# Sixteen bytes: where the high and low weight buffers of a float32r kernel begin in SBUF

## The chip, the cores and the metric

The kernel runs on one core of a Trainium2 chip. The metric is the device time of one execution in microseconds; the time before is the median of three runs, and a separate profiled execution gives the trace that is read here.

## The reference

Two transformer-like networks run one after the other on 256 tokens of width 1,024. Nearly all of the arithmetic is in plain matrix products of activations with float32 weights that are read once:

```python
def swiglu(x, w_gate, w_up, w_down):
    return (jax.nn.silu(x @ w_gate) * (x @ w_up)) @ w_down

def first_block(x, ...):
    for l in range(DEPTH):
        h = rms_norm(x, ffn1_norm[l])
        x = x + 0.5 * swiglu(h, ffn1_w_gate[l], ffn1_w_up[l], ffn1_w_down[l])
        h = rms_norm(x, mix_norm[l])
        ... = jnp.split(h @ w_in[l], SPLIT_POINTS, axis=-1)
        ...
        x = x + merged @ w_out[l]
        h = rms_norm(x, ffn2_norm[l])
        x = x + 0.5 * swiglu(h, ffn2_w_gate[l], ffn2_w_up[l], ffn2_w_down[l])
    return x

def second_block(x, c, ctx, ...):
    for i in range(DEPTH):
        ...
        if i % 2 == 0:
            y_c, y_l = even_mixer(h_c, h_l, ev_w_in[j], ev_w_out[j], ...)
        else:
            y_c, y_l = retention_mixer(h_c, h_l, od_w_in[j], od_w_out[j], ...)
        x = x + g_a * y_l
        x = x + g_m * sq_relu_mlp(modulate(rms_norm_2(x, norm_mlp_g[i]), sh_m, sc_m), mlp_w1[i], mlp_w2[i])
        ...
    return rms_norm_2(x, final_g)
```

## The kernel before, in words

A float32 product is made of three products in the type float32r, which TensorE reads at one column a step: every float32 number is split into a high part (the number rounded to float32r) and a low part (what is left), and high times high, high times low and low times high are added up in PSUM.

Weights come in pieces of 512 KB. `wload` (line 238) takes a raw buffer `wraw` and two split buffers `whi` and `wlo` from `wtile` (line 225), loads the raw piece by DMA from the queue of SyncE (line 246), and splits it: ScalarE copies it to `whi` (line 251), VectorE subtracts and writes `wlo` (line 252; a few pieces go to GpSimd). Each of the three buffers holds 1,024 float32 numbers a partition, 4,096 bytes, as 2 rows of 512 columns or as 4 rows of 256. There are four raw buffers and three of each split kind in the pool `wp`; the feed-forward and mixer stages add some of their own (`more_weights`).

Two routines multiply. In `gemm` (line 264) the weights are the moving operand, which streams through the array, and 128 columns of the activations (`hA`, `hB`, `ahi`, `alo`, `yhi`, `ylo`) are the stationary operand, which is loaded first; its three products are lines 291, 292 and 293. In `gemm_t` (line 299) 128 columns of the weights are stationary and the activations move; its products are lines 333, 334 and 335. The retention mixer has three float32r products of its own without weights (lines 1484 to 1486).

Two small tiles, `gap0` (64 bytes, line 106) and `gap1` (224 bytes, line 110), are allocated between pools and never read. With them every float32r tile begins at a multiple of 256 bytes, and since a product takes its operands at whole rows of 2,048 or 1,024 bytes or at groups of 128 columns (512 bytes), both operands of all 9,816 float32r products in the program begin at a multiple of 256.

Products in full float32 are left over in the mixers: line 1289 multiplies tiles that begin 32 bytes behind a multiple of 256 (a tile of 32 bytes, `sink2`, stands ahead of them), and line 1465 tiles at a multiple of 256.

The first 16,384 bytes of every partition are kept by the program for DMAs that GpSimd issues (their scratch memory); the tiles follow behind them.

Of the kernel before, what the change touches and what calls it, by code (L numbers as in the profile page):

```python
# [11 lines left out]
F32 = mybir.dt.float32  # L12
F32R = mybir.dt.float32r
# [86 lines left out]
class Net:  # L100
# [125 lines left out]
    def wtile(self, name, shape):  # L226

        own = {"wraw": 4, "whi": 3, "wlo": 3}[name]
        more = self.more.get(name, 0)
        i = self.turn[name] = (self.turn.get(name, -1) + 1) % (own + more)  # L230
        pool, bufs = (self.wp, own) if i < own else (self.more_pool, more)
        return pool.tile(shape, F32 if name == "wraw" else F32R, name=name, bufs=bufs)

    def more_weights(self, pool=None, **k):
        self.more_pool, self.more, self.turn = pool, k, {}
# [1373 lines left out]


# [12 lines left out]
```

## Time and profile before

| | |
|---|---|
| runs | 2446.25, 2447.65 and 2445.13 us, median 2446.25 us |
| profiled execution | 2448.74 us, of which the span from the first to the last instruction is 2447.0 us |
| mean granted TensorE clock | 0.992 of full speed |
| TensorE matmul | busy 2379.9 us, 97% of the span, 11,941 records |
| VectorE, ScalarE, GpSimd | busy 63%, 45% and 6% |
| moved by DMA | 405.85 MB, 166 GB/s over the span |

An engine's busy time counts an instruction from its start to its end. Matmuls overlap, and a matmul record is longer than the time until the next one starts, so the rate of TensorE is read here from start to start (called the pitch), in the timeline, which lists instructions in order of time.

### The profile page before, as it was taken

The numbers are of one execution on the slowest core, as the hardware profiler recorded it, in microseconds if no ns is written. First come the engines' busy times: TensorE is split into PE (matmuls) and PEld (weight loads), VectorE is DVE, ScalarE is ACT, GpSimd is POOL, SyncE is SP. The second block draws the span as 40 slices with busy tenths as digits, with TensorE's granted clock in tenths as the row PEclk, the third lists the DMA queues.
The fourth block names the chain that finished last, engine by engine and source line by source line (L and its number), as shares of the span: only waits on it lengthen the run. The fifth ranks groups of instructions, "written<-read, shape, count | busy, mean of one in ns | idle before, by whom it ended". The sixth has DMA issues, their size and how long they took to land. (4 is left out here: it accounts for less than half of the span.)

```text
span 2447.0 us, 31298 instructions
## 1 busy us (share of the span) xinstructions
PE 2379.9 (97%) x11941; PEld 1924.1 (79%) x11941; DVE 1542.1 (63%) x2237; ACT 1107.5 (45%) x1715; POOL 145.1 (6%) x175
## 2 busy tenths in 40 slices
PE   9999999999999999999999999999999999999998
PEld 7887777778788867778887767788887888887996
DVE  5775677756767557685855765555534654565665
ACT  5444664544444456554543434331424433334543
POOL 2000100110000000000000001000001110110000
PEclk9999999999999999999999999999999999999999
DMA  8775536856777554586642122645432433344664
GB/s 273 249 254 183 165 121 196 265 168 211 241 215 225 174 164 140 163 277 186 218 146 90 53 86 69 193 167 170 141 99 86 140 103 104 112 129 138 198 182 137
DMA packets 212350, 405.85 MB, mean 166 GB/s; under 512 B 14830, under 2 KB 48365, under 8 KB 211688
## 3 DMA queue, kind: packets, MB, share of 16 engines
q1 hardware_dynamic: 207416, 391.77, 50.8%
q0 software_dynamic: 3776, 9.38, 1.2%
q10 hardware_dynamic: 1008, 2.70, 0.3%
q8 instruction: 94, 1.54, 0.3%
q14 instruction: 56, 0.46, 0.1%
HBM read 401.48 MB, written 4.67 MB: 166 GB/s over the span
## 5 line engine op out<-in xcount | busy, mean ns | idle before, releaser
L252 DVE TENSOR_TENSOR wlo<-wraw,whi 128x1024 fp32r<-128x1024 f32 (+1 forms) x617 | 750.8, 1221 | 588.1 <-ACT whi L251 585.9
L251 ACT CAST whi<-wraw 128x1024 fp32r<-128x1024 f32 (+1 forms) x622 | 649.1, 1046 | 952.5 <-PE acc L293 707.7
L291 PE MATMUL acc<-whi,hA 128*128 128x512 f32 (+1 forms) x1472 | 561.0, 381 | 1.8 <-ACT hA L378 0.8
L292 PE MATMUL acc<-wlo,hA 128*128 128x512 f32 (+1 forms) x1472 | 556.9, 378 | 0.3 <-DVE wlo L252 0.3
L293 PE MATMUL acc<-whi,hA 128*128 128x512 f32 (+2 forms) x1152 | 432.5, 375 | 1.4 <-DVE hA L379 1.4
L291 PEld LDWEIGHTS acc<-whi,hA 128*128 128x128 f32 x1472 | 278.1, 189 | 61.0 <-issue 8.6
L292 PEld LDWEIGHTS acc<-wlo,hA 128*128 128x128 f32 x1472 | 278.3, 189 | 49.1 <-DVE wlo L252 1.7
L291 PE MATMUL acc<-whi,ahi 128*128 128x512 f32 x736 | 288.5, 392 | 0.0
L293 PE MATMUL acc<-whi,alo 128*128 128x512 f32 x736 | 286.8, 390 | 0.0
L292 PE MATMUL acc<-wlo,ahi 128*128 128x512 f32 x736 | 286.7, 390 | 0.0
L333 PE MATMUL acc<-hA,whi 128*128 128x512 f32 (+1 forms) x752 | 259.5, 345 | 6.4 <-ACT rl L1385 3.4
L334 PE MATMUL acc<-hA,wlo 128*128 128x512 f32 (+1 forms) x752 | 259.2, 345 | 2.4 <-POOL wlo L252 2.4
L335 PE MATMUL acc<-hB,whi 128*128 128x512 f32 (+1 forms) x752 | 257.8, 344 | 0.0
L293 PEld LDWEIGHTS acc<-whi,hA 128*128 128x128 f32 x1152 | 218.0, 189 | 40.4 <-DVE hA L379 2.0
L333 PEld LDWEIGHTS acc<-hA,whi 128*128 128x128 f32 x752 | 144.8, 193 | 25.2 <-ACT rl L1385 3.8
L291 PEld LDWEIGHTS acc<-whi,ahi 128*128 128x128 f32 x736 | 138.2, 188 | 30.2 <-issue 2.3
L334 PEld LDWEIGHTS acc<-hA,wlo 128*128 128x128 f32 x752 | 145.1, 193 | 21.4 <-issue 3.4
L293 PEld LDWEIGHTS acc<-whi,alo 128*128 128x128 f32 x736 | 138.2, 188 | 29.3 <-issue 0.4
L292 PEld LDWEIGHTS acc<-wlo,ahi 128*128 128x128 f32 x736 | 138.2, 188 | 28.1 <-issue 0.2
L335 PEld LDWEIGHTS acc<-hB,whi 128*128 128x128 f32 x752 | 144.6, 193 | 17.2 <-issue 1.4
L999 DVE SCALAR_TENSOR_TENSOR hB<-hB,cT 128x1024 f32<-128x1024 f32 x112 | 141.0, 1279 | 22.1 <-DMA hB<-in_ada_w_dram 21.8
L293 PE MATMUL acc<-whi,hB 128*128 128x512 f32 (+1 forms) x320 | 121.5, 382 | 2.5 <-DVE hB L433 2.4
(422 smaller groups left out, 2544.2 us busy)
## 6 DMA issues: line engine op xcount, KB each, us to landing
wraw<-in_mlp_w_dram SPq DMA_DIRECT2D x128, 512.0 KB, 3.8
wraw<-in_ffn_w_gate_dram SPq DMA_DIRECT2D x88, 512.0 KB, 4.2
wraw<-in_ffn_w_up_dram SPq DMA_DIRECT2D x88, 512.0 KB, 4.6
wraw<-in_ffn_w_down_dram SPq DMA_DIRECT2D x88, 512.0 KB, 4.0
wraw<-in_w_in_dram SPq DMA_DIRECT2D x84, 512.0 KB, 3.7
hB<-in_ada_w_dram SPq DMA_DIRECT2D x64, 512.0 KB, 4.9
wraw<-in_od_w_in_dram SPq DMA_DIRECT2D x64, 512.0 KB, 3.7
xA<-in_ada_w_dram SPq DMA_DIRECT2D x32, 512.0 KB, 4.4
```

The lines of the kernel that those rows point to most:

```text
L251: nc.scalar.copy(hi[sl], raw[sl])
L252: (nc.gpsimd if e & 1 else nc.vector).tensor_sub(lo[sl], raw[sl], hi[sl].bitcast(F32))
L291: nc.tensor.matmul(o, h, wh, start=kt == first, stop=False)
L292: nc.tensor.matmul(o, h, wl, start=False, stop=False)
L293: nc.tensor.matmul(o, l, wh, start=False, stop=kt == end)
L333: nc.tensor.matmul(o, wh[:, cs], xh[:, kt, ts], start=st, stop=False, skip_group_check=skew_or_pair)
L334: nc.tensor.matmul(o, wl[:, cs], xh[:, kt, ts], start=False, stop=False, skip_group_check=skew_or_pair)
L335: nc.tensor.matmul(o, wh[:, cs], xl[:, kt, ts], start=False, stop=en, skip_group_check=skew_or_pair)
L999: nc.vector.scalar_tensor_tensor(acc[tok], raw, c, acc[tok], op0=ALU.mult, op1=ALU.add)
```

## The change

`wtile` no longer hands out a whole tile for `whi` and `wlo`. It allocates 1,088 float32 numbers a partition (4,352 bytes, 17 times 256), and gives the 1,024 that begin at the fifth: 16 bytes behind the tile's start. `wraw` and all activations stay as they were. Six split buffers stand in `wp`, and every further pair in a stage's pool, so the tiles behind them move by multiples of 256. The memory for this comes from the scratch for GpSimd's DMAs, which is halved to 8,192 bytes.

```diff
         pool, bufs = (self.wp, own) if i < own else (self.more_pool, more)
-        return pool.tile(shape, F32 if name == "wraw" else F32R, name=name, bufs=bufs)
+        if name == "wraw":
+            return pool.tile(shape, F32, name=name, bufs=bufs)
+
+        t = pool.tile([128, 1088], F32R, name=name, bufs=bufs)[:, 4:1028]
+        return t.rearrange("p (k n) -> p k n", k=shape[1])
...
-    nc = bacc.Bacc("TRN2", target_bir_lowering=False, num_devices=1)
+    nc = bacc.Bacc("TRN2", target_bir_lowering=False, num_devices=1, dynamic_dma_scratch_size=8192)
```

On every engine the same instructions stand in the same order as before, with the same shapes; addresses alone differ. Of the 9,816 float32r products, 7,392 (lines 291 to 293) now have the moving operand 16 bytes behind a multiple of 256 and the stationary one at a multiple, 2,256 (lines 333 to 335) have it the other way round, and 168 (lines 1484 to 1486) are as they were.

## Rows read from the trace of the kernel before

**Rows 1.** The page: busy time of the matmul engine, and the granted clock in 40 slices.
```profile
PE   9999999999999999999999999999999999999998
PEclk9999999999999999999999999999999999999999
```
**Rows 2.** Groups by line and shape, TensorE: busy us, mean ns of one, idle before.
```profile
L291 PE MATMUL acc<-whi,hA 128*128 128x512 f32 x1248 | 495.5, 397 | 1.7 <-ACT hA L378 0.8 <-ACT kv L1157 0.4 <-ACT whi L251 0.4
L291 PE MATMUL acc<-whi,ahi 128*128 128x512 f32 x736 | 288.5, 392 | 0.0
L291 PE MATMUL acc<-whi,yhi 128*128 128x512 f32 x256 | 101.4, 396 | 0.0
L333 PE MATMUL acc<-hA,whi 128*128 128x512 f32 x400 | 158.3, 396 | 3.4 <-ACT rl L1385 3.4
L333 PE MATMUL acc<-hA,whi 128*128 128x256 f32 x352 | 101.2, 288 | 3.0 <-ACT hA L432 3.0
L291 PE MATMUL acc<-whi,hA 128*128 128x256 f32 x192 | 55.7, 290 | 0.2
L291 PE MATMUL acc<-whi,hA 128*128 128x280 f32 x32 | 9.8, 305 | 0.0
```
**Rows 3.** Windows, line 291 alone: stretch, length, PE busy (count), PEld, PEclk, DMA, GB/s.
```profile
2304.00:2346.16 42.16, 24.12 (x62) 11.64 (x62) 1.00 0.63 195
```
**Rows 4.** Timeline of TensorE, 512 columns: start, length, line, operands; seven matmuls in turn.
```profile
152.97 0.39 PE L293 MATMUL acc<-whi,alo 128*128 128x512 f32 x1
...
154.33 0.39 PE L293 MATMUL acc<-whi,alo 128*128 128x512 f32 x1
```
**Rows 5.** Timeline of TensorE, 256 columns, weights stationary; seven matmuls in turn.
```profile
2349.86 0.28 PE L335 MATMUL acc<-hB,whi 128*128 128x256 f32 x1
...
2350.58 0.28 PE L335 MATMUL acc<-hB,whi 128*128 128x256 f32 x1
```
**Rows 6.** Timeline, full float32 of line 1289, and its durations by source line.
```profile
1431.55 2.74 PE L1289 MATMUL acc<-b,b 128*128 128x512 f32 x6
L1289 PE MATMUL acc<-b,b x32: 590/592/697, 1431.6 to 1455.8; 128*128 128x512 f32 x32
```
**Rows 7.** Timeline, 280 columns, first layer: six matmuls in turn.
```profile
284.38 0.30 PE L291 MATMUL acc<-whi,hA 128*128 128x280 f32 x1
...
285.05 0.30 PE L293 MATMUL acc<-whi,hA 128*128 128x280 f32 x1
```
**Rows 8.** Timeline, 280 columns, the same place of the second layer: seventeen in turn.
```profile
922.64 0.29 PE L292 MATMUL acc<-wlo,hA 128*128 128x280 f32 x1
...
924.69 0.29 PE L293 MATMUL acc<-whi,hA 128*128 128x280 f32 x1
```
**Rows 9.** Timeline, 512 columns behind other work of TensorE: eleven matmuls in turn.
```profile
230.81 0.40 PE L292 MATMUL acc<-wlo,hA 128*128 128x512 f32 x1
...
233.14 0.40 PE L293 MATMUL acc<-whi,hA 128*128 128x512 f32 x1
```
**Rows 10.** Who waited for whom: total us, times, longest us.
```profile
ACT whi L251 <- PE acc L293: 707.7, 375, 4.9
DVE wlo L252 <- ACT whi L251: 585.9, 378, 6.0
```
**Rows 11.** Groups by shape, ScalarE and VectorE, tiles at 256 and 32 bytes behind.
```profile
L479 ACT CAST ahi<-tp 128x512 fp32r<-128x512 f32 x40 | 23.5, 587 | 16.9 <-PE tp L477 15.8
L1235 ACT COPY b<-tp 128x512 f32<-128x512 f32 x16 | 9.4, 585 | 16.9 <-PE tp L1232 16.9
L1387 DVE TENSOR_TENSOR sq<-rl 128x512 f32<-128x512 f32 x48 | 32.9, 688 | 8.2 <-ACT rl L1385 7.6
L1266 DVE TENSOR_TENSOR b<-b,b 128x512 f32<-128x512 f32 x4 | 2.7, 683 | 0.0
```
**Rows 12.** The chain that ended last, by engine; GpSimd's largest DMA (KB, us to landing).
```profile
PE 39%; issue 4%; POOL 2%; DVE 2%; ACT 1%; DMA 1%; POOLq 0%; ACTq 0%; SPq 0%; DVEq 0%
bscratch<-bonce POOLq DMA_DIRECT2D x1, 2304.0 KB, 11.2
```

## The prediction

> **What bounds the kernel now.** I read the page first. TensorE is busy in every slice of the span and its clock is granted nearly throughout [rows 1]; it is the bound, and the other engines matter only where TensorE waits for them. The waits show the opposite: ScalarE's split of a weight piece waits 707.7 us for TensorE to give a buffer back, and VectorE waits for ScalarE [rows 10]. So the supply has slack, and what one multiplication takes is what the kernel takes.
>
> The groups by shape give the counts [rows 2]. With weights moving, line 291 has 1,248 + 736 + 256 = 2,240 products of 512 columns, 192 of 256 and 32 of 280; lines 292 and 293 have the same sums, which makes 6,720, 576 and 96, together 7,392. With weights stationary, line 333 has 400 of 512 and 352 of 256; with lines 334 and 335 it is 1,200 and 1,056, together 2,256. The change touches 7,392 + 2,256 = 9,648 products. Their busy times overlap, so the price of one is read from start to start. In one dense stretch line 291 stands 62 times in 42.16 us, 186 products with its two sisters: 226.7 ns each, at a granted clock of 1.00, which is 2.4 GHz [rows 3]. The timeline says the same, 1.36 us over 6 steps [rows 4]. For 256 columns it is 0.72 us over 6 steps, 120.0 ns [rows 5]. Together 7,920 × 0.2267 + 1,632 × 0.120 and the few of 280 are some 2,004 us of the 2,447 us span. **One nanosecond on each of 9,648 products is 9.65 us**; 0.2% of the time, about what a measurement of this kernel can tell from no change, is 4.9 us, half a nanosecond each.
>
> **What a product pays above its columns.** At 2.4 GHz 512 columns are 213.3 ns and 256 are 106.7 ns, so both sizes pay the same 13.3 ns on top. Full float32 pays less: six products of line 1289 take 2.74 us to the last one's end; less that one's 0.592 us and over 5 steps this is 429.6 ns, where two steps a column are 426.7 ns: 2.9 ns on top [rows 6]. So some 10.4 ns a product belong to float32r, 100 us in all, and a change of addresses could act on them, if on anything. With them the three steady pitches are whole multiples of 6.67 ns: 34 times for 512, 18 times for 256, and 20 times for the 280 columns of the first layer (0.67 us over 5 steps, 133 ns) [rows 7]. I take from this that products fall into step with something that repeats every 6.67 ns, 16 columns, 64 bytes of a moving row. They can be out of step: the second layer runs the same 280 columns, with operands at the same places, in 2.05 us over 16 steps, 128.1 ns [rows 8], and behind other work 512 columns take 2.33 us over 10 steps, 233.0 ns, before they settle [rows 9]. The step is thus not set by addresses alone; equal addresses gave two rates.
>
> **The change, part by part.**
>
> *Splitting into buffers that begin 16 bytes later.* ScalarE and VectorE write and read the split halves at the new place. Tiles 32 bytes behind a multiple of 256 cost them nothing today: 585 ns against 587, and 683 against 688 [rows 11]. I take 0 and see no end above it but those few nanoseconds; the 707.7 us of ScalarE's waits for TensorE would cover them [rows 10].
>
> *The smaller scratch.* The queue of GpSimd, whose DMAs alone use it, has 0% of the chain that ends last [rows 12]. Its largest transfer lands in 11.2 us; if half the scratch made it wait for its own first half, at most that much would be added once, and only if its reader were late. A gain is excluded, since nothing gets shorter. I take 0.
>
> *Weights moving, 7,392 products.* Every moving operand of `gemm` shifts by the same 16 bytes, so from one product to the next nothing changes among them; what changes is how they stand to the stationary operand that is loaded meanwhile and to a boundary of 64 bytes. No row of this kernel has float32r operands at any other place than multiples of 256, so I bound it. Below: the excess over full float32 goes wholly, −10.4 ns. Above: every product loses one more step of 6.67 ns. The nearest row for a changed place is full float32: line 1289 has both operands 32 bytes behind and still pays only 2.9 ns [rows 6]. Nearer to float32r itself are the two rates of 280 columns at equal addresses [rows 7, 8], which speak for a rhythm that addresses do not set. I take 0.
>
> *Weights stationary, 2,256 products.* The activations that stream stay where they were; 128 columns to load begin 16 bytes later. The same bounds, and again 0.
>
> The sum is 0 on the profiled execution's 2448.74 us. That execution lies 2.5 us above the median of the runs, so the forecast for a median is **2446 us**, with a range of its own of 2441 to 2451.
>
> The Trainium skill, "TensorE: Matmul & The Clock Gate", section "Back-to-back issue gap", gives N/2.4 + 2.5 ns from start to start when warm. The full float32 rows agree (2.9 ns), the float32r rows do not (13.3 ns). If that rule held for float32r once its operands are out of each other's way, the change would give 9,648 × 10.8 ns, an estimate of 104 us. The same page, section "Step-by-step: what each phase is for", says that the streaming operand and the load of the stationary one have independent read ports, so that one takes nothing from the other. That speaks against any gain from setting the two apart; no row can show it here, since all pairs stand alike today.
>
> **The rivals.**
>
> *Faster: the two operands hinder each other today.* If loading 128 columns and streaming collide because both begin at the same place of 256 bytes, 16 bytes between them may take one 6.67 ns step out: 220.0 and 113.3 ns. For it: the excess is the same 13.3 ns for 512 and 256 columns, as a cost of the load or of the start would be, and full float32, which streams half as fast, does not have it. Against it: equal places gave two rates [rows 7, 8]. Its time: 9,648 × 6.67 ns = 64 us less, 2382 us; ScalarE's waits would shrink but not end [rows 10]. If the whole excess goes, which is also the rule above, 100 us less, 2346 us. Chance 0.34, of which 0.08 for the whole excess.
>
> *Slower: the shifted row no longer falls into step.* If a row has to begin at a 64-byte boundary to settle, the moving weights stay out of step: 233.0 instead of 226.7 ns, 6.3 ns on 6,720 products, 42 us: 2488 us. It decides from the first dense stretch on, in which the pitch would wander instead of standing at 226.7. For it: a step is 16 columns, and 280 columns, 17.5 such steps, are the one size that has no steady pitch in both layers, and in the first it pays 16.7 ns on top (133.3 less 116.7) instead of 13.3. If a shifted row costs one whole step everywhere, it is 64 us, 2510 us. Against it: the dense stretches find their step again from any start [rows 9]. Chance 0.30, of which 0.08 for the whole step or more.
>
> *The change does nothing that the engine sees* is the forecast itself: all addresses move alike for the moving rows. Chance 0.36.
>
> **How the numbers follow.** The three cases have 0.36, 0.34 and 0.30; the likeliest gives the time. The range goes from 2382, one step less, to 2490, out of step, and leaves out the whole excess (0.08), the whole step (0.08) and little else. Faster by over 0.2% has 0.34, within 0.2% 0.36, slower 0.30: both signs hold most of the chance, and only the forecast's own range is narrow.
>
> **What would show it.** The pitch in the dense stretch at the program's end: 226.7 ns as before is the forecast, 220 or less the first rival, 233 or wandering the second. For lines 333 to 335 120.0 ns, 113 or 127 say it for the other direction, and the two may part: then the shifted operand that moves and the one that is loaded matter differently. Lines 1484 to 1486 must stay. GpSimd's share of the chain should stay near 2% with its queue at 0. I am wrong if the pitch of the dense stretches moves by more than half a nanosecond either way.

## The result, and the profile after

The changed kernel takes 2471.25 us (median of four runs, 2470.07 to 2472.17) against 2446.95 us for the kernel before (four runs). The ratio is 1.0093, with a 95% interval of 1.0077 to 1.0110: **slower by 24 us**, clear of noise. It lies inside the stated range of 2382 to 2490, but the forecast was no change, and its own range ended at 2451.

From the page of the profile after, the rows that answer to [rows 1], [rows 10] and [rows 12]. The line numbers are four higher than before (251 is 255, 291 is 295, 333 is 337):

```profile
span 2470.4 us, 31298 instructions
PE 2405.2 (97%) x11941; PEld 1922.8 (78%) x11941; DVE 1542.3 (62%) x2237; ACT 1104.9 (45%) x1715; POOL 144.4 (6%) x175
PEclk9999999999999999999999999999999999999999
PE 39%; issue 3%; POOL 2%; DVE 1%; ACT 1%; DMA 0%; POOLq 0%; ACTq 0%; SPq 0%; DVEq 0%
L256 DVE TENSOR_TENSOR wlo<-wraw,whi 128x1024 fp32r<-128x1024 f32 (+1 forms) x617 | 750.9, 1221 | 605.9 <-ACT whi L255 601.1
L255 ACT CAST whi<-wraw 128x1024 fp32r<-128x1024 f32 (+1 forms) x622 | 647.0, 1043 | 978.9 <-PE acc L297 720.9
```

The reader is to see where the time did not go. VectorE's and ScalarE's splits take what they took, 1,221 and 1,043 ns a piece. The page of before has 1,221 and 1,046:

```profile
L252 DVE TENSOR_TENSOR wlo<-wraw,whi 128x1024 fp32r<-128x1024 f32 (+1 forms) x617 | 750.8, 1221 | 588.1 <-ACT whi L251 585.9
L251 ACT CAST whi<-wraw 128x1024 fp32r<-128x1024 f32 (+1 forms) x622 | 649.1, 1046 | 952.5 <-PE acc L293 707.7
```

Of the rest: ScalarE waits a little longer for TensorE, 720.9 us instead of 707.7; GpSimd's queue still has nothing of the chain; the clock is granted. TensorE alone grew, from 2379.9 to 2405.2 us.

Next the windows, as in [rows 3] (stretch, its length, PE busy and count of the one line asked for, PEld, PEclk, DMA, GB/s), for three dense stretches of the kernel after: weights moving with 512 columns (line 295), weights stationary with 512 (line 338) and with 256 (line 337):

```profile
1808.28:1863.18 54.90, 31.13 (x79) 14.85 (x79) 1.00 0.29 95
1564.34:1627.34 63.00, 35.46 (x90) 17.28 (x90) 1.00 0.45 144
2369.39:2414.48 45.09, 35.65 (x127) 23.82 (x127) 1.00 0.61 187
```

Each stretch runs from the start of one group of three products to the start of a later one; the count can hold one more that touches the edge. The first is 79 groups, 237 products: 54.90 / 237 = 231.6 ns. The second is 90 groups: 63.00 / 270 = 233.3 ns. The third is 127 groups: 45.09 / 381 = 118.3 ns. The same three places in the kernel before (lines 291, 335 and 333; the middle stretch is 88 groups there):

```profile
1790.66:1844.38 53.72, 30.73 (x80) 14.83 (x79) 1.00 0.29 95
1553.13:1612.98 59.85, 34.24 (x89) 16.52 (x88) 1.00 0.45 143
2346.39:2392.10 45.71, 35.94 (x127) 24.31 (x127) 1.00 0.61 185
```

They give 53.72 / 237 = 226.7, 59.85 / 264 = 226.7 and 45.71 / 381 = 120.0 ns. So in these stretches products of 512 columns became slower by 5.0 ns (weights moving) and 6.6 ns (weights stationary), and those of 256 columns *faster* by 1.6 ns. With stationary weights not every stretch of 512 columns left its pitch: 119 such products in a row from 1781.3 us on have a mean of 226.7 ns in the kernel after too. The timeline of the first stretch shows that the pitch does not stand still any more, as it did in [rows 4]:

```profile
1809.67 0.39 PE L295 MATMUL acc<-whi,ahi 128*128 128x512 f32 x1
1809.89 0.40 PE L296 MATMUL acc<-wlo,ahi 128*128 128x512 f32 x1
1810.13 0.40 PE L297 MATMUL acc<-whi,alo 128*128 128x512 f32 x1
1810.36 0.39 PE L295 MATMUL acc<-whi,ahi 128*128 128x512 f32 x1
1810.59 0.39 PE L296 MATMUL acc<-wlo,ahi 128*128 128x512 f32 x1
1810.82 0.40 PE L297 MATMUL acc<-whi,alo 128*128 128x512 f32 x1
1811.06 0.40 PE L295 MATMUL acc<-whi,ahi 128*128 128x512 f32 x1
```

Six steps take 1.39 us here instead of 1.36; the single steps are 0.22, 0.23 and 0.24; to the nanosecond they repeat as about 227, 234, 235 and 230.

Every float32r product of the program has its record in both traces, so the whole difference can be added up: the sum over a group of the times from one start to the next start on TensorE, waits included.

| products | count | before, us | after, us | difference |
|---|---|---|---|---|
| weights moving, 512 columns | 6,720 | 1594.3 | 1618.1 | +23.9 |
| weights moving, 256 columns | 576 | 77.9 | 75.8 | -2.0 |
| weights moving, 280 columns | 96 | 13.6 | 13.3 | -0.3 |
| weights stationary, 512 columns | 1,200 | 284.0 | 288.1 | +4.1 |
| weights stationary, 256 columns | 1,056 | 135.8 | 133.4 | -2.5 |
| no weights | 168 | 38.1 | 38.3 | +0.3 |

Together, before rounding, +23.4 us, and the span grew by 23.4. Nothing else has to be looked for. The 168 products without weights, which by the prediction must stay, kept their operands' places but not quite their pitch, 228.2 ns in the mean instead of 226.7: some at the start of each group are out of step, and the others stand at 226.7.

### The profile page after: what moved, and what is told of

It is laid out like the page before. It is cut to its first block, busy times and chain, and to the rows that moved or that the text cites. A ratio compares the mean times of both kernels' runs of the same rounds, so it can differ in the third digit from the quotient of the medians.

```text
span 2470.4 us, 31298 instructions
## 1 busy us (share of the span) xinstructions
PE 2405.2 (97%) x11941; PEld 1922.8 (78%) x11941; DVE 1542.3 (62%) x2237; ACT 1104.9 (45%) x1715; POOL 144.4 (6%) x175
## 5 line engine op out<-in xcount | busy, mean ns | idle before, releaser
L256 DVE TENSOR_TENSOR wlo<-wraw,whi 128x1024 fp32r<-128x1024 f32 (+1 forms) x617 | 750.9, 1221 | 605.9 <-ACT whi L255 601.1
L255 ACT CAST whi<-wraw 128x1024 fp32r<-128x1024 f32 (+1 forms) x622 | 647.0, 1043 | 978.9 <-PE acc L297 720.9
```

What stands on the lines that cost most here:

```text
L255: nc.scalar.copy(hi[sl], raw[sl])
L256: (nc.gpsimd if e & 1 else nc.vector).tensor_sub(lo[sl], raw[sl], hi[sl].bitcast(F32))
```

## The experiments

Three theories were on the table. **A (relation)**: what counts is how the moving operand stands to the stationary one; equal places let the products fall into step. **B (boundary)**: an operand must itself begin at a 64-byte boundary. **C (scratch)**: the smaller scratch costs the time. All times below are ratios to the kernel before on the same chip, with 95% intervals. In each, the dense stretch of 237 products with moving weights is read; where the edit adds lines, its line numbers shift by one or two.

**The scratch alone.** The kernel before with

```diff
-    nc = bacc.Bacc("TRN2", target_bir_lowering=False, num_devices=1)
+    nc = bacc.Bacc("TRN2", target_bir_lowering=False, num_devices=1, dynamic_dma_scratch_size=8192)
```

> The kernel before with the smaller DMA scratch alone; all float32r operands stay at multiples of 256. Theory A (the two operands of a product must begin at equal places to fall into step) and theory B (each operand must begin at a boundary of 64 bytes) both expect the pitch of before, 226.7 ns for 512 columns and 120.0 ns for 256, and the time of before within 5 us. Theory C (the scratch costs the time) expects the 24 us of the change, 2470 us.

Ratio 0.9989 (0.9977 to 1.0001). Windows of this kernel, line 291:

```profile
1786.01:1839.73 53.72, 30.73 (x79) 14.83 (x79) 1.00 0.28 94
```

53.72 us again: 226.7 ns. Theory C is out.

**One direction at a time.** The changed kernel, with the shift set by the routine that asks for the piece:

```diff
-        t = pool.tile([128, 1088], F32R, name=name, bufs=bufs)[:, 4:1028]
+        t = pool.tile([128, 1088], F32R, name=name, bufs=bufs)[:, self.off:self.off + 1024]
...
+                self.off = 4
                 hi, lo = self.wload(src, k0, m, c0, cn)
```

with `self.off = 4` in `gemm` and 0 in `gemm_t`, and the other way round.

> The change for lines 291 to 293 alone (weights that move begin 16 bytes later; weights that are loaded as the stationary operand stay at multiples of 256). Theories A and B: 512 columns at a mean of 231.6 ns and 256 columns at 116.4 ns in lines 295 to 297, and 226.7 and 120.0 ns in lines 338 to 340. From the pitches of the changed kernel: 6,720 products by +4.3 ns, 576 by -3.3 and 96 by -3.4, +26.7 us, of which some four fifths showed in the span, so 2467 to 2474 us.

Ratio 1.0081 (1.0060 to 1.0102), 2467.1 us. Windows, line 296 (moving, 237 products) and line 341 (stationary, 512 columns, 264 products):

```profile
1801.67:1856.57 54.90, 31.13 (x79) 14.85 (x79) 1.00 0.28 93
1562.30:1622.15 59.85, 34.24 (x89) 16.52 (x88) 1.00 0.44 143
```

231.6 ns where the shift is, 226.7 where it is not.

> The change for the products with stationary weights alone. Theory A: their 512 columns at 231 ns and their 256 columns at 118.4 ns, the products with moving weights at 226.7; 1,200 by +3.7 ns less 1,056 by 1.6 ns, +2.7 us, 2447 to 2452 us, within the noise of the time but not of the pitch. A narrower theory B, that only the moving row has to begin at a boundary, expects 226.7 and 120.0 ns everywhere.

Ratio 1.0011 (1.0000 to 1.0021), 2449.3 us. Windows, line 296 (moving) and line 339 (stationary, 256 columns, 381 products):

```profile
1791.79:1845.51 53.72, 30.73 (x80) 14.83 (x79) 1.00 0.28 95
2346.13:2391.22 45.09, 35.65 (x128) 23.82 (x127) 1.00 0.60 187
```

The moving products are at 226.7 ns again and the short ones with shifted stationary weights at 118.3. A shift of the operand that is merely loaded changes the rate of the row that streams, although that row begins at a multiple of 256: the narrower theory B falls here. The products of 512 columns came out at a mean of 229.5 ns (from start to start, over those that are at most 40 ns above their columns' time, so that waits are left out; the means below are taken in the same way) where 231 was expected: only part of them left their step. Their longest stretch did not (line 341, 267 products; TensorE alone, without the weight loads):

```profile
1552.42:1612.94 60.52, 34.62 (x89) 1.00 0.46 147
```

That is 226.7 ns, where the same stretch of work in the kernel after, with operands at the same places, stood at 233.3. So a difference of 16 bytes this way round has two rates for 512 columns, one step of 6.67 ns apart. The two ratios, 0.81% and 0.11%, add up to that of the change; the second by itself can hardly be told from none.

**Everything 32 bytes later.** The kernel before with

```diff
-        self.gap(pool, "gap0", 16)
+        self.gap(pool, "gap0", 24)
```

which puts all float32r operands 32 bytes behind a multiple of 256, off every 64-byte boundary but at equal places.

> The kernel before with the first gap tile 32 bytes larger: every float32r tile, weights and activations, begins 32 bytes behind a multiple of 256, so the two operands of each product stand alike and neither is at a boundary of 64. Theory A (relation): 226.7 and 120.0 ns and the time of before within 5 us. Theory B (boundary): out of step everywhere, about 231.6 and 117 ns, 7,920 by +4.2 ns less 1,632 by 2.3 ns, +29 us by the pitch, 2468 to 2476 us.

Ratio 1.0014 (1.0003 to 1.0026). Windows, line 291 (moving, 237) and line 333 (stationary, 256 columns, 381):

```profile
1790.98:1844.70 53.72, 30.73 (x79) 14.83 (x79) 1.00 0.27 95
2346.13:2391.84 45.71, 35.94 (x127) 24.31 (x127) 1.00 0.62 185
```

226.7 and 120.0 ns to the last digit; the ratio, 0.14% above 1, is within the 5 us that theory A allowed. **The relation counts, the boundary does not**: theory A stands and B is out.

**How far until the places are equal again?** The changed kernel with the split buffers 32, 64, 128 and 192 bytes behind (`8:1032`, `16:1040`, `32:1056`, `48:1072` in place of `4:1028`), and with 4 bytes (`1:1025`). There are two runs each at 32, 128, 192 and 4 bytes, and eight at 64.

> As the change, but the split buffers begin 32 bytes behind a multiple of 256. Relation with a period of 64 bytes (6.67 ns are 16 columns, 64 bytes of a moving row): still out of step, 512 columns near 231 to 234 ns and 256 near 116 to 119 ns, 2462 to 2485 us. Relation with a period of 32 bytes or less: 226.7 and 120.0 ns, time of before within 5 us.

> The split buffers begin 64 bytes behind a multiple of 256. Period of 64 bytes: back in step, 226.7 and 120.0 ns, time of before within 5 us. Period of 128 or 256 bytes: out of step, 512 columns well above 227 ns and 2462 to 2485 us.

> The split buffers begin 128 bytes behind a multiple of 256. Period of 64 or 128 bytes: in step, 226.7 and 120.0 ns, time of before within 5 us. Period of 256 bytes: out of step, 2462 to 2485 us.

The ratios are 1.0134 (1.0110 to 1.0158), 1.0042 (1.0031 to 1.0054) and 1.0117 (1.0091 to 1.0143). The pitch of 226.7 was not found again at 64 or at 128: the periods of 64 bytes, which the 6.67 ns had suggested, and of 128 are out. The time at 64, 2458.8 us, was also below the range that was given for being out of step. Windows at 32, line 295:

```profile
1813.78:1869.08 55.30, 31.20 (x79) 14.80 (x79) 1.00 0.27 93
```

At 64, line 295 (moving, 237), line 339 (stationary, 512 columns, 267 products) and line 337 (stationary, 256 columns, 381):

```profile
1798.42:1852.68 54.26, 30.66 (x80) 14.83 (x79) 1.00 0.28 94
1555.18:1617.48 62.30, 35.21 (x90) 16.73 (x89) 1.00 0.44 143
2356.53:2399.74 43.21, 35.07 (x128) 23.77 (x127) 1.00 0.64 192
```

At 128, line 295:

```profile
1807.03:1862.11 55.08, 31.16 (x80) 14.88 (x79) 1.00 0.28 92
```

That is 233.3, 229.0 and 232.4 ns for moving weights. At 64 the two directions part: 229.0 ns with moving weights, 62.30 / 267 = 233.3 with stationary ones, and 113.4 ns for 256 columns there, the lowest of any long stretch. At 128 they do not part: the mean of 512 columns is 232.6 ns both ways. If only the difference of the two starts counts, in a circle of 256 bytes, moving weights stand at +64 and stationary ones at -64. That can be tested with 192, which swaps them:

> The split buffers begin 192 bytes behind a multiple of 256. Theory A with a period of 256 bytes says that only the moving start less the stationary start counts, taken in a circle of 256: the products with moving weights then stand at -64 and those with stationary weights at +64, the reverse of the run at 64. So they swap rates: moving weights 233.3 ns for 512 columns and 113.6 for 256, stationary weights 229.2 and 117.8 ns. If each operand's own place counts, they do not swap. Time by those pitches against equal places: 6,720 by +6.0, 1,200 by +1.9, 576 by -6.1, 1,056 by -2.1, +37 us, 2475 to 2488 us.

Ratio 1.0123 (1.0105 to 1.0141). Windows at 192, line 295 (moving, 237), line 339 (stationary, 512 columns, 267) and line 337 (stationary, 256 columns, 381):

```profile
1809.05:1864.34 55.29, 31.12 (x79) 14.77 (x79) 1.00 0.28 93
1566.97:1628.11 61.14, 34.91 (x89) 16.71 (x89) 1.00 0.45 145
2373.94:2418.82 44.88, 35.44 (x128) 23.68 (x127) 1.00 0.62 186
```

They swapped: 233.3 ns moving, 229.0 stationary, 117.8 for the 256 columns. The 576 moving products of 256 columns, too scattered for a stretch, have a mean of 114.8 ns, near the 113.6 expected. So no shorter period than 256 bytes is left. That 256 is enough, the run with stationary weights alone shows: its split buffers lie 4,352 bytes, 17 times 256, apart, so that moving weights stand an even and an odd number of times 256 from the activations in turn, and all of its moving products stood at 226.7 ns in the stretch above. The period is 256 bytes.

> The split buffers begin 4 bytes, one column, behind a multiple of 256. If the relation is counted in 16-byte pieces or coarser, the start still lies in the same piece: 226.7 and 120.0 ns, time of before within 5 us. If it is counted in bytes or columns, out of step as at 16 bytes: 512 columns above 228 ns, 2460 to 2475 us.

Ratio 1.0203 (1.0184 to 1.0222), 2498.9 us: the slowest of all, and beyond the 2460 to 2475 expected. Windows, line 295:

```profile
1826.02:1882.16 56.14, 31.52 (x80) 14.87 (x79) 1.00 0.28 92
```

236.9 ns. The relation is not counted in whole pieces of 16 bytes: with moving weights one column off costs more than four.

| moving start less stationary start | 512 columns, ns | seen in |
|---|---|---|
| 0 | 226.7 | before; all 32 bytes later |
| +4 | 236.9 | weights moving |
| +16 | 231.6 | the change; moving alone |
| +32 | 233.3 | weights moving |
| +64 | 229.0 | moving at 64; stationary at 192 |
| 128 | 232.4 | weights moving |
| -64 | 233.3 | moving at 192; stationary at 64 |
| -32 | 233.3 (mean) | stationary at 32 |
| -16 | 226.7 and 233.3 | stationary alone; the change |
| -4 | 232.4 (mean) | stationary at 4 |

**A version for the short rows.** Rows of 256 and 280 columns were faster out of step, so only their weights were shifted: `self.off = 4 if cn < 512 else 0` in `gemm` and `4 if nt == 256 else 0` in `gemm_t` (96 of the 1,056 short products with stationary weights, halves of longer rows, keep equal places).

> Only the weights of products whose moving row is shorter than 512 columns begin 16 bytes later (280 and 256 columns in gemm, 256 tokens in gemm_t); all 512-column products stay at equal places. If out of step is what short rows like: 512 columns 226.7 ns, 256 columns 116.4 to 117.1 ns with weights moving and 118.3 with weights loaded, 280 columns 126.8 ns: 576 by -3.2, 1,056 by -1.6, 96 by -3.4, -3.9 us, 2441 to 2447 us, about as far as a measurement can tell. If the shift costs by itself: 2448 us or more.

Ratio 0.9993 (0.9983 to 1.0003). Windows, line 296 (512 columns, 237) and line 339 (256 columns, stationary, 381):

```profile
1790.08:1843.80 53.72, 30.73 (x79) 14.83 (x79) 1.00 0.28 94
2344.93:2390.02 45.09, 35.65 (x128) 23.82 (x127) 1.00 0.62 188
```

The pitches are what was expected, 226.7 and 118.3 ns; the time cannot be told from that of before. With the place that had given 113.4 ns (`{256: 48, 280: 4}.get(cn, 0)` in `gemm`, `16 if nt == 256 else 0` in `gemm_t`):

> All stages of 512-column products stay at equal places; 256-column products stand at -64 bytes (weights at 192 where they move, at 64 where they are loaded), 280-column ones at +16. By the rates found at those places: 576 by -6.1 ns, 960 by -6.3, 96 by -3.3, -9.9 us: 2435 to 2442 us, faster than both kernels. If the -64 rate of the stationary run does not carry over to moving weights: -6.4 us, 2439 to 2445.

Ratio 0.9993 (0.9982 to 1.0005), 2444.86 us. Windows, line 339 (256 columns, stationary, 381):

```profile
2339.23:2384.10 44.87, 35.69 (x127) 23.77 (x127) 1.00 0.63 189
```

117.8 ns instead of 113.4, so the 2435 to 2442 us expected were not reached: the same places gave another rate than in the run at 64, as equal places gave two for 280 columns [rows 7, 8] and -16 two for 512. What decides between two rates at one place was not found. The moving products of 256 columns went to a mean of 114.9 ns. No version here is measurably faster than the kernel before.

## Why the prediction was wrong

*What bounds the kernel, and what costs nothing: right.* TensorE's pitch is the kernel's time: the float32r products make up the 23.4 us by which the span grew. Splitting into shifted buffers cost 0 and so did the scratch, the latter by a run of its own.

*Weights moving and weights stationary, both taken at 0: this step failed.* Measured are +23.9 and +4.1 us on the products of 512 columns, less 4.8 us on the shorter ones. The step rested on two readings. The first was that full float32 with both operands 32 bytes behind pays no more [rows 6]. But there both operands are shifted alike; by the run with everything 32 bytes later that is a difference of 0, and the row had nothing to say about a difference of 16. The second was that 280 columns ran at two rates at equal places [rows 7, 8], from which the prediction concluded that addresses do not set the rhythm. They do not set it alone, but it hangs on how the two places stand to each other: at equal places every dense stretch read had 226.7 ns, and of nine other differences only -16 showed that pitch at all, in some of its stretches; the others gave 229.0 to 236.9. The bounds, -10.4 and +6.67 ns, did hold for the change (+5.0 in the dense stretch of moving weights, +6.6 in that of stationary ones), though not for 4 bytes (+10.2).

*The slower rival* had the mechanism in part: out of step, the pitch wanders. Its cause, a row that has to begin at a 64-byte boundary, is refuted by the run with everything 32 bytes later, in step off the boundary, and by those at 64 and 128, out of step on it. Its size was 42 us. Measured are 23.9 us for the 6,720 products, because the dense pitch was 231.6 and not the 233.0 of [rows 9], and because the mean over all of them is 3.6 ns, less than the 5.0 of a dense stretch. Between products at most 40 ns above their columns the mean went up by 4.3 ns, so part of the rest lies in the products with a longer time behind them: 310 before and 300 after, 137.2 us and 131.1. Why these shrank is not shown. It also left out the rows of 256 and 280 columns (-4.8 us) and the stationary 512 (+4.1), which cancel by chance.

*The faster rival*, that the two operands hinder each other at equal places, is half refuted: for 512 columns nothing that was tried is faster than the 226.7 of equal places, for 256 they are the worst but one: only 4 bytes with moving weights, at a mean of 122.9 ns, were slower than 120.0. The rival's 113.3 ns did come up as a steady pitch with weights stationary at 64 bytes (113.4); at 16 bytes the means were 116.4 and 118.3.

The Trainium skill, "TensorE: Matmul & The Clock Gate", section "Step-by-step: what each phase is for", says that loading the next stationary operand takes no SBUF read bandwidth from the product that runs. Whether it does here, the runs do not show, but the two are not independent in time: moving the loaded operand alone, by 16 bytes, changed the rate of rows that had not moved, 120.0 to 118.3 ns for 256 columns. The section "Back-to-back issue gap" of that page gives N/2.4 + 2.5 ns for products on their own, 215.8 ns for 512 columns and 109.2 for 256, and says that a stream of loads and products is spaced by both, a condition that the prediction left out; no float32r stretch read here reached it at any place (226.7 and 113.4 at best).

## What to carry to other kernels

Where float32r products of 512 columns bound a kernel, let the moving and the stationary operand begin at the same place in a circle of 256 bytes; the place itself made no difference between the two that were tried, 0 and 32 bytes. Shifting the weight buffers and not the activations, by 4 to 192 bytes, lost 0.4 to 2% here, so look at the pitch in a dense stretch after every change of the memory layout. A row of the trace bears on a change only if it differs in what the change changes: ask of an operand pair how the two stand to each other, not where each of them stands.

## What was not expected of the hardware

The period of 256 bytes, when the steady pitches of before (226.7, 120.0 and 133.3 ns) were multiples of 6.67 ns, the time of 64 bytes of a moving row. The steady products keep that rhythm through the whole execution: in the trace of before the remainders of some 8,000 starts by a fitted 6.666655 ns agree across waits and other work between them (the length of their mean vector is 0.92, where 1 is full agreement and 0 none). Two of the other pitches are whole numbers of it again, 233.3 ns (35 steps) and 113.3 (17), while 229.0, 231.6 and 236.9 are not. That out of step long rows lose and short rows gain: at a difference of 16 bytes +5.0 ns for 512 columns, -1.6 to -3.3 for 256. And that one column, 4 bytes, costs most, 10.2 ns a product of 512 columns with moving weights. What in TensorE or SBUF has this rhythm, and what decides between two rates at one place, the runs don't show.
